# Eight of twelve modulation blocks of a hybrid SSD and gated-MLP layer: from TensorE products to VectorE multiplies with a running sum

## The chip, the cores and the metric

The kernel runs on one core of one Trainium2 chip. The metric is the device time of one execution in microseconds (us), and of several executions the median. The engines are TensorE (PE in the profile; its weight loads are shown apart, as PEld), VectorE (DVE), ScalarE (ACT), GpSimd (POOL), and SyncE (SP), which here only issues DMAs.

## What is computed

One layer of a flow-matching backbone on 1024 latent tokens and 128 context tokens with 1024 channels: a Mamba-2 scan, a spatial gating branch, their merge, and a convolutional FFN. The change concerns the modulation: a condition vector for each of the two kinds of token goes through SiLU and one matrix of 1024 x 6144. The result is cut into six rows of 1024.

```python
mod_ctx = jax.nn.silu(c_ctx)[None, :] @ w_mod[i] + b_mod[i]
mod_lat = jax.nn.silu(c) @ w_mod[i] + b_mod[i]
...
shift1, scale1, gate1, shift2, scale2, gate2 = jnp.split(mod[:, None, :], 6, axis=-1)
h = _rmsnorm(x, lp["norm_mix_pre"]) * (1 + scale1) + shift1
mix, hf, hb = _token_mixer(h, h0_f, h0_b, lp)
x = x + gate1 * _rmsnorm(mix, lp["norm_mix_post"])
h = _rmsnorm(x, lp["norm_ffn_pre"]) * (1 + scale2) + shift2
x = x + gate2 * _rmsnorm(_conv_ffn(h, on_grid, lp), lp["norm_ffn_post"])
```

## The kernel before

All products of large matrices run on TensorE as three products of fp32r parts (high x high, high x low, low x high). Weights come in halves of 128x512 (`wr`, three buffers), each of which ACT casts to its high part (`wh`, L83) and DVE subtracts to its low part (`wl`, L84). A class `Weights` loads and splits them ahead of their use, in the order of one list.

The program has four parts in time: the input projection and the scan, the spatial gating branch, the branch projections with the merge and the output projection, and the FFN. The modulation is cut into twelve blocks of 512 columns. Blocks 0 to 3 (shift1, scale1) are computed at the very start; the change leaves them alone. Blocks 4 to 11 (gate1, shift2, scale2, gate2) are computed in the spatial gating branch, in `mod_step` (L903). It goes as follows, for a block b:

- four DMAs of 512 KB bring its weights (`wmod`, L207) into buffers of the tag `xm`, of which there are four;
- 16 products (L224) with the condition as the stationary operand (`cs`, 32 columns, two of them used) leave partial sums in four groups of rows of a PSUM bank, and ACT copies them out (`modrow`, L228);
- for shift2 and scale2 (`mod_cols`) four transposes (L235) bring the columns onto the partitions, and small DVE operations add the groups up and apply bias and norm weight;
- for the gates (`mod_gate`) two products with a selecting matrix (L253) add the groups up into a row for each kind of token, DVE applies bias and norm weight on one partition (L254, L255), and DMAs write the row to a scratch tensor, `gate_scr`.

Around it, for each half h of the channels of v: one gate unit (72 products into `gps`, three token blocks), then nine token tiles by `v_tile` (L853), each of 24 products into one of the three banks of the pool `pg`, an ACT copy out (L862) and a DVE statistic (L863). The eight halves of the weights of v stay in place for all nine tiles (six of them in `vwh` and `vwl`). Behind every third tile of the second half, `layernorm` normalises three tiles of v (L875). Then come eight u units (`u_unit`, L877), each of three token blocks: 24 products into `gps`, six into `psg` (L881), two DVE operations (L884, L887). L842 is a short product for the branch's bias, early in the stage.

The program is recorded in the order of the code, and a list scheduler then places the instructions of each engine by its own estimates of their durations. So the order in which an engine executes differs from the code's. An engine executes its instructions strictly in the order placed, and an instruction that waits holds up all behind it. SP issues all DMAs, in one such order.

## Time and profile before

| what | value |
|---|---|
| median of 3 runs | 2494.64 us (2494.25 to 2495.19) |
| span of the profiled execution | 2495.0 us |
| mean granted TensorE clock | 0.994 |
| moved by DMA | 322.36 MB, 129 GB/s |

The profiled execution is described by its span alone; it lies 0.4 us above the median. The page gives the busy time of each engine, the chain of work that ended last, and groups of instructions by source line; other views of the trace are the timeline of an engine, tables of windows, and the chain within a window. All times of instructions are in us from the start of the span. A group's row ends with its count, its busy time in us, the mean of one in ns, and the idle time ahead of it with what ended that.

### The profile page before, as it was taken

Reading aid. Unit: us, or ns where it says so; the run is one execution under the profiler, and the core shown is the slowest. Engines: PE = TensorE matmul, PEld = TensorE weight load, DVE = VectorE, ACT = ScalarE, POOL = GpSimd, SP = SyncE. Lnnn points to the kernel's source line nnn. Section 1 sums busy time; section 2 is a strip of 40 time slices with the busy share of each in tenths; the row PEclk is TensorE's granted clock in tenths of the full one; section 3 lists DMA queues with packets and bytes.
Section 4 is the critical chain, followed back from the end, with each engine's and each line's share of the span. In section 5 each row is a group of like instructions: output and inputs, shape, how many; then the busy total and the mean of one; then the engine's idle time right before and its main releaser. Section 6 shows DMA issues by size and latency. Waiting matters only on the chain.

```text
span 2495.0 us, 37933 instructions
## 1 busy us (share of the span) xinstructions
PE 2456.4 (98%) x14237; PEld 2281.7 (91%) x14237; DVE 1795.4 (72%) x3042; ACT 1113.4 (45%) x2124; POOL 26.1 (1%) x82
## 2 busy tenths in 40 slices
PE   7989999999999999999999999999999999999998
PEld 4989999999999997789999998999999999998877
DVE  4768988878868883243455747558999989998554
ACT  4545655655544552211344536444333333334443
POOL 0000000000000000000000000000000000000000
PEclk8999999999999999999999999999999999999999
DMA  6134334434433434531445747542222121214673
GB/s 255 34 99 147 121 125 142 130 95 127 144 94 112 146 118 169 199 105 63 137 153 169 241 155 242 165 147 76 70 72 70 64 72 56 70 62 132 215 246 130
DMA packets 204168, 322.36 MB, mean 129 GB/s; under 512 B 19320, under 2 KB 113400, under 8 KB 203984
## 3 DMA queue, kind: packets, MB, share of 16 engines
q1 hardware_dynamic: 203984, 319.93, 39.2%
q8 instruction: 112, 1.84, 0.3%
q14 instruction: 72, 0.59, 0.1%
HBM read 277.33 MB, written 42.52 MB: 128 GB/s over the span
## 4 chain that ended last, share of the span: by engine, by line
PE 94%; DMA 3%; DVE 1%; ACT 1%; issue 0%; SPq 0%; POOL 0%; DVEq 0%; POOLq 0%; ACTq 0%
PE gps L294 11%; PE gps L296 11%; PE gps L295 11%; PE pup L294 7%; PE pup L295 7%; PE pup L296 7%; PE fo L1132 3%; PE fo L1133 3%; PE fo L1134 3%; PE yo L733 2%; PE pbs L294 2%; PE pbs L295 2%; PE pbs L296 2%; PE yd L737 2%; PE pv L860 1%; PE pv L858 1%
## 5 line engine op out<-in xcount | busy, mean ns | idle before, releaser
L84 DVE TENSOR_TENSOR wl<-wr,wh 128x512 fp32r<-128x512 f32 x544 | 372.2, 689 | 269.4 <-ACT wh L83 256.9
L83 ACT CAST wh<-wr 128x512 fp32r<-128x512 f32 x544 | 333.9, 619 | 492.7 <-PE pup L295 121.6
L294 PE MATMUL gps<-hh,wh 128*128 128x384 f32 x1512 | 518.3, 343 | 0.2 <-ACT pad L349 0.2
L296 PE MATMUL gps<-hh,wl 128*128 128x384 f32 x1512 | 514.2, 340 | 0.0
L295 PE MATMUL gps<-hl,wh 128*128 128x384 f32 x1512 | 513.4, 340 | 0.0
L1120 DVE SCALAR_TENSOR_TENSOR acc<-U,fpar,acc 128x960 f32<-128x960 f32 (+1 forms) x352 | 444.1, 1266 | 16.0 <-ACT acc L1113 8.2
L295 PE MATMUL pup<-h2l,wh 128*128 128x384 f32 x1056 | 353.1, 334 | 0.0
L294 PE MATMUL pup<-h2h,wh 128*128 128x384 f32 x1056 | 352.9, 334 | 0.0
L296 PE MATMUL pup<-h2h,wl 128*128 128x384 f32 x1056 | 352.4, 334 | 0.0
L294 PEld LDWEIGHTS gps<-hh,wh 128*128 128x128 f32 x1512 | 284.7, 188 | 6.7 <-issue 5.9
L296 PEld LDWEIGHTS gps<-hh,wl 128*128 128x128 f32 x1512 | 284.5, 188 | 4.8 <-issue 4.8
L295 PEld LDWEIGHTS gps<-hl,wh 128*128 128x128 f32 x1512 | 284.7, 188 | 4.2 <-issue 4.2
L294 PEld LDWEIGHTS pup<-h2h,wh 128*128 128x128 f32 x1056 | 198.2, 188 | 1.3
L295 PEld LDWEIGHTS pup<-h2l,wh 128*128 128x128 f32 x1056 | 198.2, 188 | 1.3
L296 PEld LDWEIGHTS pup<-h2h,wl 128*128 128x128 f32 x1056 | 198.2, 188 | 0.0
L1102 ACT COPY U<-pup 128x384 f32<-128x384 f32 (+1 forms) x132 | 58.4, 442 | 225.2 <-PE pup L296 225.2
L665 ACT ACTIVATE R<-R,nb 128x128 f32<-128x128 f32 x288 | 93.2, 391 | 130.4 <-DMA R<-acs_scr 120.9
L1132 PE MATMUL fo<-wh,gh 128*128 128x512 f32 x384 | 148.0, 396 | 0.9 <-ACT wh L83 0.9
L1133 PE MATMUL fo<-wh,gl 128*128 128x512 f32 x384 | 148.3, 396 | 0.0
L1134 PE MATMUL fo<-wl,gh 128*128 128x512 f32 x384 | 139.9, 396 | 0.0
L294 PE MATMUL pbs<-ysh,wh 128*128 128x384 f32 x384 | 129.7, 338 | 3.7 <-ACT wh L83 2.2
L296 PE MATMUL pbs<-ysh,wl 128*128 128x384 f32 x384 | 129.5, 337 | 0.1
(302 smaller groups left out, 3939.8 us busy)
## 6 DMA issues: line engine op xcount, KB each, us to landing
wr<-in_w_dn SPq DMA_DIRECT2D x132, 256.0 KB
wr<-in_w_in SPq DMA_DIRECT2D x130, 256.0 KB
R<-acs_scr SPq DMA_DIRECT2D x64, 512.0 KB
wmod<-in_w_mod SPq DMA_DIRECT2D x48, 512.0 KB
wr<-in_w_bs SPq DMA_DIRECT2D x96, 256.0 KB
wr<-in_w_up SPq DMA_DIRECT2D x90, 256.0 KB
EP<-acs_scr SPq DMA_DIRECT2D x128, 128.0 KB
wr<-in_w_bu SPq DMA_DIRECT2D x48, 256.0 KB
```

The lines of the kernel that those rows point to most:

```text
L83: self.nc.scalar.copy(hi, w)
L84: self.nc.vector.tensor_tensor(lo, w, hi.bitcast(F32), op=ALU.subtract)
L294: PE.matmul(ps, lhsT=wh, rhs=xh, start=first and k == 0, stop=False)
L295: PE.matmul(ps, lhsT=wh, rhs=xl, start=False, stop=False)
L296: PE.matmul(ps, lhsT=wl, rhs=xh, start=False, stop=last and k == n - 1)
L665: S.activation(r, r, AF.Identity, bias=nb[:, c, col:col + 1])
L733: PE.matmul(yo[:, d, i, :], lhsT=H[:, k, d, :], rhs=CT[:, 128 * c:128 * c + 128], start=True, stop=True)
L1102: S.copy(u[:, a // 64:b // 64, 1:65], src.rearrange("p (r c) -> p r c", c=64))
L1120: tap = V.scalar_tensor_tensor(av[:, r0:r1], u[:, r0 + dy - 1:r1 + dy - 1, dx:dx + 64], w[i], av[:, r0:r1], op0=ALU.mult, op1=ALU.add)
L1132: PE.matmul(outs[c][h], lhsT=mh[:, cs_], rhs=wh, start=k == 0, stop=False)
L1133: PE.matmul(outs[c][h], lhsT=ml[:, cs_], rhs=wh, start=False, stop=False)
L1134: PE.matmul(outs[c][h], lhsT=mh[:, cs_], rhs=wl, start=False, stop=k == NFF - 1)
```

## The change

The weights of blocks 4 to 11 are given to the kernel transposed: 32 tiles of 128 output channels (on the partitions) by 1024 inputs (`w_modt`), 512 KB each. The two conditions are brought onto all 128 partitions by one broadcast DMA of 1 MB into `cc` and go through SiLU there, on ACT. Each of 64 dot products per partition group is then one DVE instruction: weight tile times condition, with a running sum over the 1024 inputs into one column of `modc` (L247 of the new program). A step (`mod_step`) does one tile, that is two such multiplies, and issues the load of the tile four steps on. One step stands behind every v tile (18 steps) and one behind every token block of the u units, until 32 are done. After each eight, `mod_finish` applies bias and norm weight to eight columns at once; for the two gates, `mod_rows` transposes 16 columns by one product (L259) and writes them to `gate_scr`.

```diff
-    def mod_gate(tile_, ps, pt, b, hs, sel):
...
+    def mod_dot(wt, junk, cc, m):
+        for s in range(2):
+            V.scalar_tensor_tensor(junk if s == 0 else wt, wt, 1.0, cc[:, s, :], op0=ALU.mult, op1=ALU.mult,
+                                   accum_out=modc[:, m, s:s + 1])
+
+    def mod_finish(c0, w=None, one=0.0):
+        m = modc[:, c0:c0 + 8, :]
+        V.tensor_tensor(m, m, par[:, P_BM + c0:P_BM + c0 + 8].unsqueeze(2).to_broadcast([128, 8, 2]), op=ALU.add)
+        if w is not None:
+            V.scalar_tensor_tensor(m, m, one, par[:, w:w + 8].unsqueeze(2).to_broadcast([128, 8, 2]), op0=ALU.add, op1=ALU.mult)
+
+    def mod_rows(ps, room, gi, c0):
+        PE.transpose(ps[:16, :128], modc[:, c0:c0 + 8, :].rearrange("p k s -> p (k s)"), ident)
+        row = room[:16, :128]
+        S.copy(row, ps[:16, :128])
+        for s in range(2):
+            SP.dma_start(gate_scr[2 * gi + s:2 * gi + s + 1, :].rearrange("o (k m) -> (o k) m", m=128), row[s:16:2, :])
...
-    cond_cols(up)
-    sel = up.tile([128, 2, 128], F32, name="sel")
-    SP.dma_start(sel, A["sel"])
+    cc = up.tile([128, 2, 1024], F32, name="cc")
+    SP.dma_start(cc.rearrange("p s k -> p (s k)"), A["cond"].to_broadcast([128, 2048]))
+    S.activation(cc, cc, AF.Silu)
+    junk = rp.tile([128, 1024], F32, tag="gate", name="mjunk")
     mods = []
+    def mod_load1():
+        m = len(mods)
+        if m < 32:
+            wt = xm(f"wmt{m}")
+            SP.dma_start(wt, A["w_modt"][m])
+            mods.append(wt)
...
+            mod_dot(mods[m], junk, cc, 16 + m)
+            mod_load1()
...
         for c in range(NC):
-            if c % 2 and nm < 8 or h == 0 and c == 0:
-                mod_step()
-                mods.append((4 + nm, mod_load(xm, 4 + nm)))
-                nm += 1
             v_tile(h, c, parts)
+            mod_step()
...
-    nc = _bacc.Bacc("TRN2", target_bir_lowering=False, num_devices=1)
+    nc = _bacc.Bacc("TRN2", target_bir_lowering=False, num_devices=1, dynamic_dma_scratch_size=1024)
```

The last pair of lines makes room in on-chip memory for `cc`. The packed parameters grow by 16 columns, and comments are gone from the new text, so line numbers differ by 7 from L84 of the new program on and by more further down.

The order of the instructions is the same in both programs up to the start of the spatial gating branch. From there on it differs, at these places.

**The start of the branch, on DVE and ACT.** These are the rows of DVE from the end of the scan on, before (`vwl` and `wl` are low parts of the weights of v, k tile by k tile; `sb` is the branch's bias):

```order
L592 TENSOR_TENSOR ssq<-ssq,z_9473 128x1152
L215 MEMSET cs 128x256
L84 TENSOR_TENSOR vwl<-wr_9432,vwh 128x512
L84 TENSOR_TENSOR vwl<-wr_9529,vwh 128x512
L84 TENSOR_TENSOR vwl<-wr_9561,vwh 128x512
L844 SCALAR_TENSOR_TENSOR sb<-prs_9593,par,sb 128x128 x4
L84 TENSOR_TENSOR vwl<-wr_9669,vwh 128x512
L844 SCALAR_TENSOR_TENSOR sb<-prs_9599,par,sb 128x128 x4
L84 TENSOR_TENSOR vwl<-wr_9701,vwh 128x512
```

And the rows of DVE at the same place in the changed program:

```order
L85 TENSOR_TENSOR vwl<-wr_9561,vwh 128x512
L851 SCALAR_TENSOR_TENSOR sb<-prs_9593,par,sb 128x128 x4
L851 SCALAR_TENSOR_TENSOR sb<-prs_9599,par,sb 128x128 x4
L247 SCALAR_TENSOR_TENSOR mjunk,modc<-wmt_9613,cc 128x1024
L85 TENSOR_TENSOR vwl<-wr_9676,vwh 128x512
L85 TENSOR_TENSOR vwl<-wr_9708,vwh 128x512
L247 SCALAR_TENSOR_TENSOR wmt_9613,modc<-wmt_9613,cc 128x1024
L247 SCALAR_TENSOR_TENSOR mjunk,modc<-wmt_9615,cc 128x1024
L85 TENSOR_TENSOR vwl<-wr_9715,vwh 128x512
L85 TENSOR_TENSOR wl_9730<-wr_9719,wh_9729 128x512
```

The split of the fourth k tile, and every split behind it, now has multiplies ahead of it. On ACT the changed program has these rows there:

```order
L84 CAST vwh<-wr_9561 128x512
L908 ACT_TABLE_LOAD
L908 ACTIVATE cc<-cc 128x2048
L84 CAST vwh<-wr_9676 128x512
L84 CAST vwh<-wr_9708 128x512
```

The SiLU of `cc`, which needs the broadcast, stands ahead of the cast of the fourth k tile; before, a SiLU of 16 columns of `par` stood there, whose input had been there since the start of the program.

**The same place on SP.** The DMAs issued before, from the first modulation weights on (`gb_scr` takes gate rows out, `wsT`, `sb` and `sel` are small operands, `wr` the weights of v):

```order
L207 DMA wmod_9734<-in_w_mod 128x1024
L604 DMA gb_scr<-gt 128x384 x2
L207 DMA wmod_9736<-in_w_mod 128x1024
L207 DMA wmod_9738<-in_w_mod 128x1024
L836 DMA wsT<-in_sgu_w 128x1024
L838 DMA sb<-in_sgu_b 128x1024
L900 DMA sel<-in_sel 128x256
L71 DMA wr_9669<-in_w_v 128x512
```

And those of the changed program:

```order
L916 DMA wmt_9613<-in_w_modt 128x1024
L916 DMA wmt_9615<-in_w_modt 128x1024
L916 DMA wmt_9617<-in_w_modt 128x1024
L916 DMA wmt_9619<-in_w_modt 128x1024
L611 DMA gb_scr<-gt 128x384
L843 DMA wsT<-in_sgu_w 128x1024
L845 DMA sb<-in_sgu_b 128x1024
L907 DMA cc<-in_cond 128x2048
L72 DMA wr_9676<-in_w_v 128x512
```

One more load of modulation weights and the broadcast of `cc` now stand ahead of the load of the fourth k tile.

**The second half of v, on DVE.** The splits of its weights stood before behind statistics and single rows of the gates; this is the changed program from the first of these splits on:

```order
L85 TENSOR_TENSOR vwl<-wr_10038,vwh 128x512
L247 SCALAR_TENSOR_TENSOR wmt_10220,modc<-wmt_10220,cc 128x1024
L247 SCALAR_TENSOR_TENSOR mjunk,modc<-wmt_10251,cc 128x1024
L870 BN_STATS stat<-vtok 128x6
L85 TENSOR_TENSOR vwl<-wr_10095,vwh 128x512
L85 TENSOR_TENSOR vwl<-wr_10127,vwh 128x512
L247 SCALAR_TENSOR_TENSOR wmt_10251,modc<-wmt_10251,cc 128x1024
L247 SCALAR_TENSOR_TENSOR mjunk,modc<-wmt_10291,cc 128x1024
L85 TENSOR_TENSOR vwl<-wr_10134,vwh 128x512
L253 TENSOR_TENSOR modc<-modc,par 128x16
L85 TENSOR_TENSOR wl_10149<-wr_10138,wh_10148 128x512
```

Multiplies now stand between the splits as well as ahead of them. The scheduler has moved the multiplies forward against the code: all 64 stand ahead of the last `layernorm`, so none is left among the u units.

## The prediction

> **What bounds the kernel now.** I read the page first: busy time by engine, then the chain that ended last.

> ```profile
> span 2495.0 us, 37933 instructions
> ...
> PE 2456.4 (98%) x14237; PEld 2281.7 (91%) x14237; DVE 1795.4 (72%) x3042; ACT 1113.4 (45%) x2124; POOL 26.1 (1%) x82
> ...
> PE 94%; DMA 3%; DVE 1%; ACT 1%; issue 0%; SPq 0%; POOL 0%; DVEq 0%; POOLq 0%; ACTq 0%
> ```

> TensorE carries 94% of the chain, so a microsecond taken off TensorE counts unless a wait takes its place. The profiled execution spans 2495.0 us and the median of the runs is 2494.64 us: nothing but 0.4 us separates them, and I subtract from the median. The share of busy time is an average, so the next view is the table of windows over the stage that is edited: from the first product of v (956.65) to the end of the first spatial product (1103.76), and the eight u units behind it.

> ```profile
> 956.65:1103.76 147.11, 147.11 (x828) 109.30 (x828) 48.15 (x95) 30.41 (x52) 2.55 (x3) 1.00 0.51 176
> 1103.76:1218.00 114.24, 114.24 (x706) 114.24 (x705) 44.46 (x76) 16.43 (x30) 0.00 (x0) 1.00 0.22 73
> ```

> Columns: length, then busy time of PE, weight load, DVE, ACT, POOL, granted clock, DMA share, GB/s. TensorE is never idle in either stretch. DVE works 48 of 147 us. That is the room into which the change moves the modulation.

> **What is removed.** Eight blocks of modulation leave TensorE. The chain inside the window 955 to 1110 (155 us) gives their shares, and three pieces of it show what one block does to its neighbours.

> ```profile
> by line: PE pv L860 22.1%; PE pv L858 21.9%; PE pv L859 21.6%; PE pm L224 10.9%; PE gps L295 5.4%; PE gps L294 5.3%; PE gps L296 5.3%; PE pmt L253 2.2%; PE pm L253 2.2%; PE prs L842 1.2%; PE pmt L235 1.1%; PE psg L881 0.9%
> ...
> 1042.63 1.86 PE pm L224 x32
> 1044.49 0.43 PE pv L858
> 1044.92 0.24 PE pv L859
> ```

> L224, L253 (twice) and L235 are 10.9 + 2.2 + 2.2 + 1.1 = 16.4% of 155 us, **25.4 us**. Each run of L224 also delays the product behind it, 0.43 us in place of 0.23: 19 such places, **3.8 us**. Removed: **29.2 us**. The two products that are added (the 16-row transposes of L259) have the nearest row in L235: 1.1% of 155 us over 16 records is 0.11 us each, with 0.2 us behind them at most; I take **0.3 us** for both, between 0.2 and 0.6.

> **The cover that goes at the start.** The first part of the stage was short of weights, and modulation filled the hole. Timelines of DVE, ACT, PE and SP:

> ```profile
> 957.88 0.69 DVE L84 TENSOR_TENSOR vwl<-wr,vwh 128x512 fp32r<-128x512 f32 x1 [2.02 <-ACT vwh L83]
> ...
> 967.63 0.68 DVE L84 TENSOR_TENSOR vwl<-wr,vwh 128x512 fp32r<-128x512 f32 x1
> ...
> 966.31 0.62 ACT L83 CAST vwh<-wr 128x512 fp32r<-128x512 f32 x1 [6.93 <-DMA wr<-in_w_v]
> ...
> 956.30 0.33 PE L295 MATMUL gps<-hl,wh 128*128 128x384 f32 x1
> 956.47 0.33 PE L296 MATMUL gps<-hh,wl 128*128 128x384 f32 x1
> ...
> 960.77 0.39 PE L858 MATMUL pv<-vwh,hh 128*128 128x512 f32 x1
> 961.00 0.39 PE L859 MATMUL pv<-vwh,hl 128*128 128x512 f32 x1
> ...
> 964.42 1.07 PE L224 MATMUL pm<-wmod,cs 128*32 128x256 f32 x16
> 965.42 1.98 PE L842 MATMUL prs<-wsT,cst 128*128 128x512 f32 x4
> ```

> The third k tile was split at 958.6, the fourth only at 967.6, because its load landed at about 966.2. A product of v starts 0.23 us behind the one before it (960.77, 961.00; 0.2275 over many), one of a projection unit 0.17 (956.30, 956.47; 0.1735). With three v tiles open TensorE has 27 products of 0.2275 us (956.65 to 962.8) and L842 (1.9 us): dry at **964.7** once L224 is gone.

> The fourth k tile also comes later. ACT's cast of it now stands behind the SiLU of cc, which waits for cc's transfer. KB ahead of the point that matters, by the issues of 950 to 980:

> ```profile
> wmod<-in_w_mod SPq DMA_DIRECT2D x5, 512.0 KB
> wr<-in_w_v SPq DMA_DIRECT2D x8, 256.0 KB
> yssd_scr<-X SPq DMA_DIRECT2D x1, 576.5 KB
> gb_scr<-gt SPq DMA_DIRECT2D x3, 192.0 KB
> wsT<-in_sgu_w SPq DMA_DIRECT2D x1, 512.0 KB
> sb<-in_sgu_b SPq DMA_DIRECT2D x1, 512.0 KB
> sel<-in_sel SPq DMA_DIRECT2D x1, 128.0 KB
> ...
> 954.00:966.30 12.30, 12.30 (x70) 8.64 (x69) 1.99 (x3) 3.55 (x7) 0.00 (x0) 1.00 1.01 355
> ```

> Before, through the fourth k tile: 576.5 + 3 x 512 + 2 x 192 + 512 + 512 + 128 + 256 = 3904 KB, at full DMA share. After, through cc (1024 KB): 576.5 + 4 x 512 + 192 + 512 + 512 + 1024 = 4864 KB. The 960 KB more, 983,000 bytes, take 2.8 us at 355 GB/s: cc lands at about 969.0. A SiLU of 2048 columns is 1.97 us, extrapolated from these two:

> ```profile
> L591 ACT ACTIVATE z<-X 128x1024 f32<-128x1024 f32 x16 | 16.9, 1058 | 9.7 <-DVE X L590 9.7
> ...
> L520 ACT ACTIVATE pad<-z 128x1152 f32<-128x1152 f32 x16 | 18.7, 1172 | 1.3
> ```

> Then the cast, 0.62 us. TensorE resumes at 971.7: a stall of **7.0 us**. Its bounds are 4 us (cc as early as the old load) and 10 us (a broadcast of 1 MB at half the rate). Afterwards TensorE needs 5 x 9 x 0.2275 = 10.2 us for the five remaining k tiles; DVE's splits, with multiplies between them, reach the last at about 981, in step with it. One more cover is lost behind the three tiles, where L253 ran while ACT emptied the first bank: **0.4 us**, most of a 0.59 us copy.

> A long pause also costs clock, as the start of this kernel shows:

> ```profile
> 18.00:20.00 2.00, 0.36 (x2) 0.30 (x2) 0.79 (x3) 2.00 (x5) 0.00 (x0) 0.99 1.02 416
> 20.00:22.00 2.00, 2.00 (x8) 1.77 (x6) 1.14 (x4) 1.83 (x4) 0.00 (x0) 0.50 1.04 416
> 22.00:24.00 2.00, 1.76 (x7) 1.42 (x7) 1.03 (x3) 0.00 (x0) 0.86 (x1) 0.66 1.03 410
> ```

> After a stretch with TensorE 0.36 of 2 us busy, the granted clock was 0.50 for 2 us and 0.66 for the next 2. Lost are 0.50 x 2 + 0.34 x 2 = **1.7 us**; bounds 0 and twice that.

> **What is added on DVE.** 64 multiplies with a running sum, 128x1024. No row has the sum. The nearest:

> ```profile
> L590 DVE TENSOR_TENSOR X<-X,z 128x1024 f32<-128x1024 f32 x16 | 19.5, 1218 | 0.1
> ...
> L521 DVE SCALAR_TENSOR_TENSOR z<-pad,z 128x1152 f32<-128x1152 f32 x16 | 21.6, 1352 | 1.2 <-ACT pad L520 1.2
> ...
> 969.26 1.28 DVE L84 TENSOR_TENSOR vwl<-wr,vwh 128x512 fp32r<-128x512 f32 x2
> ...
> 20.60 0.19 ACT L337 ACTIVATION_READ_ACCUMULATOR xj<-x 128x1 f32 x1
> 20.69 1.05 ACT L337 ACTIVATE xj<-x 128x1024 f32<-128x1024 f32 x1
> ```

> L521 is the same operation without a sum, 1.17 ns a column, like the plain product of L590: **1.22 us** for 1024. Two in a row overlap by 0.09 us (1.28 for two of 0.69). On ACT a sum adds a read that moves the next start by 0.09 us (20.60 to 20.69). I take 1.22 + 0.09 = **1.31 us**; lower bound 1.13 (overlapped, sum free), upper 1.50 (1.22, plus the whole 0.19 us read, plus 0.09 for the wait between the two of a pair). 64 x 1.31 = 84 us into 99 us of idle DVE: it fits, but only just, because the stage gets shorter.

> So DVE's row order is added up from 971.0, with 0.69 us a split or statistic:

> ```profile
> L863 DVE BATCH_NORM_STATS2 stat<-vtok 128x6 f32<-128x512 f32 x18 | 12.4, 692 | 46.2 <-ACT vtok L862 46.2
> ...
> L875 DVE TENSOR_SCALAR vtok<-vtok,mv,rv 128x1024 f32<-128x1024 f32 x9 | 6.8, 808 | 3.0 <-POOL rv L265 3.0
> ```

> Two points decide. The eighth k tile of v's second half stands behind 35 multiplies, 15 splits and 9 statistics: 45.9 + 16.6 + 0.5 = 63 us, at 1034. TensorE wants it at 981.9 + 0.4 + 1.7 + six v tiles of 5.46 (24 products) + 0.2 + a gate unit of 12.5 (72 products) + 4.8 (seven k tiles) = 1034. No loss. The last normalised tile of vtok stands behind all 64, 19 splits, 18 statistics, 9 times 0.81, 4 us of small ones and a wait of about 1 us for POOL, 1092 to 1093; TensorE wants it for the third block of the first u unit at 1092.4. I take **0.5 us**. Behind that DVE is half idle again (44 of 114 us). The 32 loads of weights are 512 KB each as before, and every wait on the SP queue is for a DVE row already passed. The room for DMA descriptors that the program gives up belongs to no queue that the page lists; I price it at nothing from either side.

> **The sum.** 29.2 - 7.0 - 1.7 - 0.4 - 0.3 - 0.5 = **19.3 us** saved; 2494.64 - 19.3 = **2475 us**.

> **The rivals.**

> *DVE becomes the bound* (slower). Above 1.31 us, each 0.01 us of a multiply adds 0.64 us at the last vtok tile, on which TensorE waits. At 1.31 + 19.3/64 = 1.61 us the gain is gone; beyond it the kernel is slower than before. If the second fp32 source costs a second pass of 1.07 us (1024 columns at 1.04), a multiply is 2.38 us, 68 us more: 2543 us. Against it: L521 and L590 have two fp32 sources at full rate, and L863, a reduction, takes for 512 columns what a split of 512 takes (0.69 us). Only the sum is unseen. Chance 0.10. [...]

> *The stall at the start is longer*: cc's transfer, a broadcast, or loads queued behind it take another 5 to 8 us. For it: the DMA share is 1.01 there. Against: sb is a broadcast too, and the rate held. 2480 to 2485 us, chance 0.15.

> *The stall hardly appears*, because cc lands with the first weights: 29.2 - 4 - 0.7 = 24.5 us, 2470 us. Chance 0.08.

> *The gain is given back* at later transfers, or TensorE did not lose what the chain says:

> ```profile
> 1361.07 4.22 DMA yrs<-yssd_scr
> ...
> 1366.82 6.08 DMA wr<-in_w_bs
> ```

> These waits of the whole chain end on loads released by buffers that come free in program order, so they should move up with the rest. About 2494 us, chance 0.05.

> **How the numbers follow.** Forecast 0.62, with 2471 to 2480 as its own range. The range of 2468 to 2489 takes in the longer stall and a multiply of up to 1.5 us (12 us later, 2487). A difference of 0.2%, 5 us, is about what a measurement of this kernel can tell from none: faster 0.85 (0.62 + 0.15 + 0.08), same 0.05, slower 0.10.

> **What would show it.** The multiply's mean in the group of L247, with its read of the sum (1.2 to 1.4). TensorE idle ahead of the fourth k tile, 6 to 8 us, released by ACT, and a granted clock of 0.5 behind it. TensorE not waiting for DVE at L259 or at the first u unit; a wait there in tens of microseconds would mean the first rival. u units at the old 14.6 us each and later stages earlier by one constant. It would be wrong if TensorE idled in the v tiles at large.

## The result, and the profile after

| | before | after |
|---|---|---|
| time, median of 4 runs each, us | 2494.91 (2494.25 to 2499.63) | 2475.29 (2471.90 to 2481.27) |
| ratio, 95% interval | | 0.9921 (0.9905 to 0.9937) |
| the edited stage in the profiled run, us | 258.90 | 239.56 |

The kernel is 19.6 us faster, by 0.8%. The forecast of 2475 us held. The profiled execution of the changed kernel is its slowest (2481.27 us, span 2479.3). Its page has the same shape as before; DVE now works 75% of the span:

```profile
span 2479.3 us, 37397 instructions
...
PE 2428.8 (98%) x13951; PEld 2271.1 (92%) x13951; DVE 1854.7 (75%) x3150; ACT 1110.4 (45%) x2118; POOL 27.0 (1%) x82
...
PE 89%; DMA 5%; DVE 3%; ACT 1%; issue 1%; SPq 1%; POOL 0%; DVEq 0%; POOLq 0%; ACTq 0%
```

Spans are a poor measure of this edit: the profiled executions of the kernels shown here reach the first product of v anywhere between 954.5 and 963.2 us, for work ahead of it that is the same or nearly so. I therefore measure the edited **stage**, from the first product of v to the end of the last spatial product. First the table of windows over the stage, before and after. Columns: length, busy time of PE, weight load, DVE, ACT and POOL, granted clock, DMA share, GB/s.

```profile
956.65:1215.55 258.90, 258.90 (x1518) 221.09 (x1518) 90.19 (x166) 44.41 (x76) 2.55 (x3) 1.00 0.38 131
```

```profile
960.82:1200.38 239.56, 232.64 (x1232) 212.77 (x1232) 150.27 (x275) 41.69 (x70) 3.48 (x3) 0.99 0.44 145
```

The stage lost 258.90 - 239.56 = **19.3 us**, and DVE gained 60 us of work (90.2 to 150.3, after losing its own part of the old modulation). Two things in the second row are new: TensorE idles 239.56 - 232.64 = **6.9 us**, and the clock is not 1.00. The spans differ by 15.7 us only, since the profiled execution of the changed kernel enters the stage 4.2 us later (960.82, not 956.65) and needs 0.6 us less behind it.

Where TensorE idles is told by its own timeline in the changed kernel, by the chain of waits from 955 to 985 us (start, duration, what) and by the timelines of DVE and of ACT there:

```profile
969.20 1.98 PE L849 MATMUL prs<-wsT,cst 128*128 128x512 f32 x4 [2.05 <-DMA wsT<-in_sgu_w]
975.77 0.79 PE L865 MATMUL pv<-vwh,hh 128*128 128x512 f32 x1 [4.59 <-ACT vwh L84]
```

```profile
962.14 11.14 DMA cc<-in_cond
973.30 1.91 ACT cc L908
975.21 0.52 ACT vwh L84
```

```profile
970.51 2.16 DVE L851 SCALAR_TENSOR_TENSOR sb<-prs,par,sb 128x128 f32<-128x128 f32 x8 [7.77 <-DMA sb<-in_sgu_b]
975.24 1.23 DVE L247 SCALAR_TENSOR_TENSOR mjunk<-wmt,cc 128x1024 f32<-128x1024 f32 x1 [2.57 <-ACT cc L908]
```

```profile
973.30 1.91 ACT L908 ACTIVATE cc<-cc 128x2048 f32<-128x2048 f32 x1 [9.98 <-DMA cc<-in_cond]
975.12 1.70 ACT L84 CAST vwh<-wr 128x512 fp32r<-128x512 f32 x3
```

The cast of the fourth weight tile (L84, which is L83 of the kernel before) starts when the SiLU of cc ends, and the SiLU when cc has landed. TensorE takes up the fourth tile 14.95 us after the first product of v; 27 products of 0.2275 us and the 1.9 us of prs fill 8.05 of these. The stall is **6.9 us** (forecast 7.0). As idle time it shows in two pieces: 2.05 us ahead of prs, where TensorE waits for wsT, and 4.59 us for the cast; 0.28 us more, a wait for a bank, stand 28 us into the stage. During the second piece, at about 974.2, the granted clock is halved:

```profile
973.00:975.00 2.00, 0.00 (x0) 0.00 (x0) 0.00 (x0) 1.70 (x1) 0.00 (x0) 0.81 1.02 387
975.00:977.00 2.00, 1.23 (x3) 1.04 (x4) 1.76 (x4) 1.82 (x4) 0.00 (x0) 0.50 0.07 25
977.00:979.00 2.00, 2.00 (x6) 1.51 (x6) 2.00 (x5) 0.00 (x0) 0.00 (x0) 0.50 0.46 98
979.00:981.00 2.00, 2.00 (x6) 1.57 (x5) 2.00 (x4) 0.62 (x1) 0.00 (x0) 0.50 0.82 238
981.00:983.00 2.00, 2.00 (x10) 1.60 (x9) 2.00 (x4) 0.62 (x1) 0.00 (x0) 0.99 0.75 277
```

Six products in 2 us at half clock, ten at full clock. From 975.77, where TensorE resumes, to 981.05 twelve products start, most of them 0.427 us apart; at 0.2275 us they would fill 2.73 of these 5.28 us. The half clock costs 2.55 us, or **2.6 us** in round numbers. Last, the multiply, in the groups of DVE between 960 and 1095 us (busy, mean ns, idle before and what ended it), and two rows of DVE's timeline:

```profile
L247 DVE SCALAR_TENSOR_TENSOR mjunk<-wmt,cc 128x1024 f32<-128x1024 f32 x32 | 39.0, 1220 | 2.6 <-ACT cc L908 2.6
L247 DVE SCALAR_TENSOR_TENSOR wmt<-wmt,cc 128x1024 f32<-128x1024 f32 x32 | 38.9, 1215 | 0.2
...
L247 DVE DVE_READ_ACCUMULATOR wmt<-wmt,cc 128x1 f32 x32 | 2.6, 82 | 0.0
```

```profile
978.75 1.22 DVE L247 SCALAR_TENSOR_TENSOR mjunk<-wmt,cc 128x1024 f32<-128x1024 f32 x1
979.89 0.08 DVE L247 DVE_READ_ACCUMULATOR mjunk<-wmt,cc 128x1 f32 x1
```

A multiply lasts 1.22 us and the next instruction starts 1.14 us behind its start (978.75 to 979.89). The read of the sum, 0.08 us, stands at that same moment and delays nothing.

### The profile page after: what moved, and what is told of

Its sections match the earlier page's. It is cut to its first block, busy times and chain, and to the rows that moved or that the text cites. A ratio compares the mean times of both kernels' runs of the same rounds, so it can differ in the third digit from the quotient of the medians.

```text
span 2479.3 us, 37397 instructions
## 1 busy us (share of the span) xinstructions
PE 2428.8 (98%) x13951; PEld 2271.1 (92%) x13951; DVE 1854.7 (75%) x3150; ACT 1110.4 (45%) x2118; POOL 27.0 (1%) x82
## 4 chain that ended last, share of the span: by engine, by line
PE 89%; DMA 5%; DVE 3%; ACT 1%; issue 1%; SPq 1%; POOL 0%; DVEq 0%; POOLq 0%; ACTq 0%
PE gps L301 10%; PE gps L302 10%; PE gps L303 10%; PE pup L302 7%; PE pup L301 7%; PE pup L303 7%; PE fo L1152 4%; PE fo L1154 4%; PE fo L1153 4%; PE pbs L301 2%; PE pbs L303 2%; PE pbs L302 2%; PE yo L740 2%; PE yd L744 2%; DMA R<-acs_scr 2%; PE pv L865 1%
## 5 line engine op out<-in xcount | busy, mean ns | idle before, releaser
L84 ACT CAST wh<-wr 128x512 fp32r<-128x512 f32 x544 | 333.8, 619 | 473.8 <-PE pup L302 121.6
## 6 DMA issues: line engine op xcount, KB each, us to landing
wr<-in_w_dn SPq DMA_DIRECT2D x132, 256.0 KB, 2.8
wr<-in_w_in SPq DMA_DIRECT2D x130, 256.0 KB, 2.8
R<-acs_scr SPq DMA_DIRECT2D x64, 512.0 KB, 4.4
wr<-in_w_bs SPq DMA_DIRECT2D x96, 256.0 KB, 3.5
wr<-in_w_up SPq DMA_DIRECT2D x90, 256.0 KB, 2.6
EP<-acs_scr SPq DMA_DIRECT2D x128, 128.0 KB, 3.2
wmt<-in_w_modt SPq DMA_DIRECT2D x32, 512.0 KB, 3.8
wr<-in_w_bu SPq DMA_DIRECT2D x48, 256.0 KB, 3.0
```

Of the source, the lines that this page charges most:

```text
L84: self.nc.scalar.copy(hi, w)
```

## The experiments

Two theories were open. **One**: what the change gains less than the 29 us of modulation is all lost at the start of the stage, through the order of the loads, and DVE costs nothing. **Rivals**: TensorE had less to lose than the chain said; the transfers would hold TensorE in any order; DVE is as near to its bound as the forecast had it. The table has the stage, the start of the fourth tile's products behind the first product of v, the stretches of half clock in the first 30 us by the trace's record of the granted clock, and the time (one run, except where a range or an interval is given in the text). The kernel before was timed again beside them: 2494.9 and 2495.5 us as medians, and 2500.2 us in the one run beside "multiplies twice".

| kernel | stage us | fourth tile | half clock | time us |
|---|---|---|---|---|
| before | 258.9 | 10.3 | none | 2494.9 |
| after | 239.6 | 15.0 | 6.8 | 2475.3 |
| cc early | 236.1 | 12.2 | 3.4 | 2477.7 |
| late loads | 234.0 | 9.7 | none | 2468.7 |
| cc early, late loads | 235.2 | 7.9 | 3.4 | 2474.2 |
| cc early, loads behind all | **229.3** | 7.9 | none | **2466.2** |
| filler in the pause | 237.3 | 14.4 | none | 2475.1 |
| no modulation | 231.2 | 8.6 | none | 2464.7 |
| no sum | 237.4 | 14.0 | 3.4 | 2476.2 |
| multiplies twice, free order | 237.8 | 15.0 | 3.4 | 2481.4 |
| half of them twice, order forced | 261.4 | 14.8 | 3.4 + 3.4 | 2501.9 |

**No modulation.** What is there to gain?

```diff
-    cc = up.tile([128, 2, 1024], F32, name="cc")
-    SP.dma_start(cc.rearrange("p s k -> p (s k)"), A["cond"].to_broadcast([128, 2048]))
-    S.activation(cc, cc, AF.Silu)
+    V.memset(modc[:, 16:48, :], 0.5)
...
-            mod_dot(mods[m], junk, cc, 16 + m)
-            mod_load1()
...
-    for _ in range(NXM):
-        mod_load1()
```

> Leaves out the eight modulation blocks: no loads of their weights, no cc, no multiplies; their results are 0.5 throughout. Theory A (29.2 us of TensorE's stage were modulation and 0.3 us come back as two small products; what the changed kernel gains less goes to the start): stage 258.9 - 28.9 = 230 us, 229 to 232, no wait of TensorE at the start. Rival B (TensorE did not lose what the chain says, and the stall is elsewhere): stage 236 to 240 us, as in the changed kernel.

```profile
954.54:1185.76 231.22, 230.15 (x1232) 210.95 (x1231) 78.33 (x140) 38.31 (x68) 2.55 (x3) 1.00 0.22 72
```

231.2 us, with 1.1 us of TensorE idle in it: 27.7 us less than before, 28.7 without the idle time. Theory A. TensorE did lose what the chain said, within 0.5 us, and 8.3 us of it are missing in the changed kernel.

**cc early.** The tile of cc moves to a pool that lasts, and its load and SiLU are tied behind steps 13 and 15 of the scan. `queue_behind` orders issues on one engine, without a wait; `marks` holds the instructions to stand behind, of the scan and, for the first multiply, the last one of the branch's bias (`sb`).

```diff
-    SP.dma_start(cc.rearrange("p s k -> p (s k)"), A["cond"].to_broadcast([128, 2048]))
-    S.activation(cc, cc, AF.Silu)
+    cload = SP.dma_start(cc.rearrange("p s k -> p (s k)"), A["cond"].to_broadcast([128, 2048]))
+    queue_behind(cload, marks[13, "SP"])
+    silu = S.activation(cc, cc, AF.Silu)
+    queue_behind(silu, marks[15, "ACT"])
...
+            if m == 16 and s == 0:
+                queue_behind(dot, marks["sb"])
```

> cc is loaded and put through SiLU during the scan, behind step 13's loads; everything else stays where it is in the changed kernel, the four first loads of modulation weights too. Stage = first product of v to last product of the spatial gating (239.6 us in the changed kernel, 258.9 before). Theory A (the fourth weight tile of v is late because ACT's cast of it stands behind cc's transfer and its SiLU): without them 1024 KB less are ahead, 2.9 us at 355 GB/s, and no SiLU of 1.9 us stands before the cast, so the product of the fourth tile starts about 4 us sooner, 11 us behind the first product of v in place of 15.0, and the pause is too short for the half clock (2.6 us): stage 232 to 236 us. Rival B (the transfers share one rate, so something else that is loaded there holds TensorE as long): the fourth tile starts 14 to 15 us behind the first product and the stage stays at 239 to 240 us.

The timeline of TensorE in this kernel:

```profile
969.11 3.68 PE L853 MATMUL prs<-wsT,cst 128*128 128x512 f32 x4 [2.36 <-DMA wsT<-in_sgu_w]
972.59 0.52 PE L869 MATMUL pv<-vwh,hh 128*128 128x512 f32 x1
...
975.75 0.50 PE L871 MATMUL pv<-vwl,hh 128*128 128x512 f32 x1 [1.48 <-DVE vwl L85]
```

The stage is 236.1 us, just outside what theory A gave (232 to 236), and far from rival B's 239. The fourth tile starts 2.8 us sooner, not 4. What I had left out: the first 2.4 us of the pause are a wait for wsT, behind the same four loads of modulation weights. That wait was enough for 3.4 us of half clock, and prs took 3.68 us in place of 1.98. A little later TensorE waits 1.48 us for the low part of the fourth tile: DVE's split of it stands behind the first multiply (1.14 us). So DVE is not quite free there once cc is out of the way.

**Late loads.** cc stays; the four first loads of modulation weights (2048 KB) go behind the fourth tile of v.

```diff
-    for _ in range(NXM):
-        mod_load1()
...
+        if h == 0:
+            for _ in range(NXM):
+                queue_behind(mod_load1(), W.issued[v_at[0] + 3])
```

> Only the four first loads of modulation weights are moved, behind the fourth weight tile of v; cc stays where it is in the changed kernel. 2048 KB less are ahead of cc, 5.9 us at 355 GB/s. Theory A (the data ahead on the queue sets the stall): the product of the fourth tile starts 9 to 10 us behind the first product of v in place of 15.0, the half clock is gone, stage 231 to 234 us. But the multiplies then start no sooner than in the changed kernel while TensorE is 8 us ahead: if DVE's margin is only the 7 us that its waits for TensorE showed, TensorE waits up to 2 us for DVE at the first u unit. Rival B (the SiLU and its table load alone hold the cast, whatever is loaded): fourth tile at 13 to 15 us, stage 238 to 240 us.

TensorE's waits in the first 30 us of the stage:

```profile
966.42 0.50 PE L865 MATMUL pv<-vwh,hh 128*128 128x512 f32 x1 [1.69 <-ACT vwh L84]
...
974.16 0.50 PE L865 MATMUL pv<-wh,hh 128*128 128x512 f32 x1 [1.31 <-ACT wh L84]
...
979.28 0.50 PE L865 MATMUL pv<-vwh,hh 128*128 128x512 f32 x1 [0.43 <-ACT vtok L869]
```

Theory A: the fourth tile 9.7 us behind the first product, no half clock, 234.0 us. So the bytes ahead of the load on the queue set this stall, whether they are cc (15.0 to 12.2 us without its 1024 KB and its SiLU) or weights (15.0 to 9.7 us without their 2048 KB). No wait for DVE appeared. What is left (3.4 us of idle) are 1.7 us for the fourth tile itself, whose cast still stands behind cc and its SiLU, 1.3 for a later tile and 0.4 for a bank.

**cc early, late loads.** Both, the four loads behind the sixth tile of v.

```diff
+                queue_behind(mod_load1(), W.issued[v_at[0] + 5])
```

> As the run with cc early, and the first four loads of modulation weights (2048 KB) stand behind the sixth weight tile of v on the queue of SP. Theory A: no stall of TensorE for the fourth tile, no half clock; the stage loses the 7.5 us of the stall and 2.6 us of half clock of the changed kernel: 229 to 231 us, TIME about 2465 us, ratio to the kernel before 0.988. DVE starts its multiplies 2 to 5 us sooner, so the margin at the last normalised tile stays. Rival B (DVE becomes late because the weights come late, or the stall comes back elsewhere in the first v tiles): stage 235 to 240 us, 2470 to 2475 us.

Ratio to the kernel before 0.9912 (0.9898 to 0.9925): not separable from the change itself. The stall for the fourth tile is gone (7.9 us), yet the stage is 235.2 us: rival B, and ACT's timeline names the place.

```profile
977.61 1.96 ACT L84 CAST wh<-wr 128x512 fp32r<-128x512 f32 x3 [6.47 <-DMA wr<-in_w_v]
984.36 0.62 ACT L84 CAST wh<-wr 128x512 fp32r<-128x512 f32 x1 [4.80 <-DMA wr<-in_w_in]
984.88 1.55 ACT L873 COPY vtok<-pv 128x512 f32<-128x512 f32 x3
```

The 2 MB now stand ahead of the seventh tile, so its cast waits 6.5 us. Then a cast for the next gate unit waits 4.8 us on ACT with the copies of finished v tiles queued behind it, and TensorE for their banks.

**cc early, loads behind all.** As the last, with the four loads behind all eight tiles of v's first half and the two of the next gate unit.

```diff
+                queue_behind(mod_load1(), W.issued[v_at[0] + 9])
```

> As the run with cc early and late loads, but the first four loads of modulation weights stand behind all eight weight tiles of v's first half and the two of the next gate unit, not behind the sixth. In that run the 7th tile's cast waited 6.5 us for its transfer behind 2048 KB of modulation weights, and a copy of a v tile 4.8 us behind a cast for the gate unit. Theory A (the queue's order alone made those waits): no wait of TensorE for weights in the first half of v; stage 228 to 231 us, TIME 2466 to 2469 us. Theory B (DVE's margin is only 7 us, and the multiplies start as late as in the changed kernel, 14 us behind the first product, while TensorE is 10 us ahead): a wait of TensorE for DVE of 2 to 4 us in the second half of v or at the first u unit; stage 231 to 234 us. Rival C (the rate of the transfers keeps TensorE short whatever the order): 235 us and more.

```profile
960.96:1190.28 229.32, 229.32 (x1232) 211.25 (x1232) 149.46 (x275) 38.61 (x68) 2.55 (x3) 1.00 0.45 146
```

TensorE is busy for the whole stage at a clock of 1.00, with DVE's 149 us of work beside it. 2466.16 us, ratio 0.9877 (0.9860 to 0.9893): below the interval of the change, so this version beats both kernels. Theory B, a wait for DVE, did not come. The stage is 10.2 us shorter than the change's, which is the cost of the start: 6.9 us of idle TensorE and 3.3 us more of busy time, 2.6 of them at half clock.

**Filler in the pause.** Is the half clock made by the pause? Four products more, of the same result, keep TensorE at work there.

```diff
+        for _ in range(3):
-        PE.matmul(ps, lhsT=ones, rhs=wsT[:, 4 * hb:4 * hb + 4, :], start=True, stop=True)
+            PE.matmul(ps, lhsT=ones, rhs=wsT[:, 4 * hb:4 * hb + 4, :], start=True, stop=True)
```

> The product of the row sums of the spatial weights is made three times in each half, four products of about 1 us more, with the same result; they stand where TensorE waits for the fourth weight tile. Theory A (the half clock behind the pause comes from the pause itself): TensorE resumes at the same time as in the changed kernel, 15.0 us behind the first product of v, at full clock, and the stage is 2.6 us shorter, 237 us. Rival B (the half clock comes from something else there, such as the transfers): the granted clock is 0.5 for 7 us all the same, stage 239 to 240 us. Rival C (the filler is too long and delays the fourth tile): stage above 240 us.

First two rows of TensorE's timeline, then the windows from 970 to 976 us:

```profile
966.30 5.42 PE L850 MATMUL prs<-wsT,cst 128*128 128x512 f32 x12 [1.87 <-DMA wsT<-in_sgu_w]
972.52 0.50 PE L866 MATMUL pv<-vwh,hh 128*128 128x512 f32 x1 [0.80 <-ACT vwh L84]
```

```profile
970.00:972.00 2.00, 1.71 (x4) 0.41 (x3) 0.55 (x3) 1.96 (x2) 0.00 (x0) 1.00 1.03 389
972.00:974.00 2.00, 1.48 (x6) 1.05 (x6) 2.00 (x7) 1.58 (x3) 0.00 (x0) 1.00 0.08 29
974.00:976.00 2.00, 1.49 (x7) 1.11 (x7) 2.00 (x5) 0.00 (x0) 0.00 (x0) 1.00 0.25 24
```

Theory A: the clock stays at 1.00, with the transfers at 389 GB/s (387 in the pause of the changed kernel, from 973 to 975), and the stage is 2.2 us shorter, of which the fourth tile explains 0.5 at most (14.4 us, not 15.0). Here the pause makes the half clock: 1.00 with it filled, 0.50 behind it without.

**No sum.** Does the running sum cost anything?

```diff
-            V.scalar_tensor_tensor(junk if s == 0 else wt, wt, 1.0, cc[:, s, :], op0=ALU.mult, op1=ALU.mult,
-                                   accum_out=modc[:, m, s:s + 1])
+            V.scalar_tensor_tensor(junk if s == 0 else wt, wt, 1.0, cc[:, s, :], op0=ALU.mult, op1=ALU.mult)
...
+    V.memset(modc[:, 16:48, :], 0.5)
```

> The 64 multiplies are made without the running sum; the sums are left out and the eight blocks' values are 0.5 before bias and norm weight. Theory A (the sum costs only a read that starts behind its own multiply and lies beside the next one's start): without it the starts of two multiplies in a row are 1.12 to 1.15 us apart, as with it (1.145). Rival B (the read delays the next start by its 0.08 us): 1.06 to 1.08 us. Rival C (the sum slows the pass itself): a multiply below 1.15 us in place of 1.22. In all three the stage stays at 239 to 240 us, since DVE isn't late.

```profile
992.31 1.23 DVE L247 SCALAR_TENSOR_TENSOR wmt<-wmt,cc 128x1024 f32<-128x1024 f32 x1
993.45 1.22 DVE L247 SCALAR_TENSOR_TENSOR mjunk<-wmt,cc 128x1024 f32<-128x1024 f32 x1
```

Over 37 such pairs the median from start to start is 1.136 us; with the sum it is 1.144 (36 pairs). The duration is the same, 1.22 us. Theory A: the sum costs 0.01 us. The stage, 237.4 us, fell outside the 239 to 240 that I had written: its stall was 1 us shorter and its half clock 3.4 us in place of 6.8, and neither concerns the sum.

**DVE, twice.** First a forced order: the first condition's multiply is made twice, and the last block's first normalised tile stands behind all 96 multiplies.

```diff
-            V.scalar_tensor_tensor(junk if s == 0 else wt, wt, 1.0, cc[:, s, :], op0=ALU.mult, op1=ALU.mult,
-                                   accum_out=modc[:, m, s:s + 1])
+            for _ in range(2 - s):
+                marks["dot"] = V.scalar_tensor_tensor(junk if s == 0 else wt, wt, 1.0, cc[:, s, :], op0=ALU.mult, op1=ALU.mult,
+                                                      accum_out=modc[:, m, s:s + 1])
...
+            if c == 6:
+                queue_behind(norm, marks["dot"])
...
+            if h and c == 8:
+                while mod_step.n < 32:
+                    mod_step()
```

> The multiply of the first condition is made twice (32 more multiplies, 36.6 us of DVE at 1.145 us), and the last block's first normalised tile of vtok stands behind all of them on DVE. Theory A (DVE is the next bound behind a margin of some 7 us: 3.6 and 0.3 us of waits for TensorE and 3.2 us from the last normalisation to its use): TensorE waits for DVE about 29 us at the third block of the first u unit; stage 269 us, slower than the kernel before (258.9 us). That is the first rival of the prediction with its point of decision: 29.8 us more DVE work was to undo the gain. Rival B (DVE's work hides wherever it stands, since DVE is half idle in the u units): stage 240 to 243 us.

The timelines of TensorE and DVE at the third block of the first u unit:

```profile
1127.28 2.05 PE L892 MATMUL psg<-wsT,vtok 128*128 128x128 f32 x8 [21.21 <-DVE modc L255]
```

```profile
1125.17 1.22 DVE L249 SCALAR_TENSOR_TENSOR wmt<-wmt,cc 128x1024 f32<-128x1024 f32 x1
...
1126.32 0.81 DVE L884 TENSOR_SCALAR vtok<-vtok,mv,rv 128x1024 f32<-128x1024 f32 x1
```

The product waits 21.2 us and starts when the tile is normalised (1127.13; the profile names a small DVE operation of that moment as the releaser), and the kernel is slower than before: stage 261.4 us, 2501.9 us. The size that I gave, 29 us, was too large. The last of the three tiles that the product needs came 36.0 us later than in the changed kernel (164.5 behind the first product of v, not 128.5). There TensorE wants it only at 136.6, a room of 8.1 us, and here TensorE had other products until 143.4. In the wait the clock was halved too (0.95 on average over the stage, 0.99 in the changed kernel's); it came back 4.35 us behind the end of the wait, a stretch that the table's first 30 us leave out.

Then all multiplies twice, 73 us more on DVE, and no order forced:

```diff
+            if s == 1:
+                for d in range(2):
+                    V.scalar_tensor_tensor(junk, wt, 1.0, cc[:, d, :], op0=ALU.mult, op1=ALU.mult, accum_out=modc[:, m, d:d + 1])
```

> Both multiplies of every step are made twice (64 more, 73 us of DVE), with no order forced: 71 of the 128 stand ahead of the last normalised tile of vtok, 57 lie between the u units' own operations. Theory A (where DVE's work stands decides, not how much it is): 7 multiplies more ahead of the last normalisation are 8 us, of which 3.6 us fill a wait for TensorE and 8 us is the room up to the product that wants it, so nothing is late there; in a u unit 7 multiplies of 1.145 us and 5.7 us of its own are 13.9 of 14.1 us. Stage 239 to 242 us. Rival B (DVE too full in the u units: each spatial block's result waits behind a multiply and TensorE for its bank): the u units grow by 1 to 3 us each, stage 248 to 263 us. Rival C (73 us of work without room): stage above 290 us.

```profile
960.17:1197.92 237.75, 231.09 (x1231) 212.01 (x1231) 217.28 (x399) 41.27 (x69) 2.55 (x3) 0.99 0.44 142
```

DVE is busy 217 of 238 us and the stage is no longer than the change's. Theory A, a little below its range, mostly because the half clock was 3.4 us. The time of that one run, 2481.4 us, is high, and so is the 2500.2 us of the kernel before beside it. Behind the stage it has 1281.7 us, 2.8 more than the changed kernel; 1.65 of them are a wait of TensorE for a split on DVE, 39 us behind the stage. Whether the added multiplies, the last of which ends 2.3 us behind the stage, cause it was not tried. So 37 us of DVE work ahead of one tile cost the stage 22, and 73 us that lie mostly between the u units cost it nothing.

## Why the prediction was right

| term | forecast us | measured us |
|---|---|---|
| modulation removed, less the two products added | 28.9 | 29.6 (258.90 - 229.32) |
| stall at the start | 7.0 | 6.9 |
| half clock and lost bank cover | 2.1 | 3.3 (the rest of 10.2) |
| DVE late | 0.5 | 0 |
| net | 19.3 | 19.3 |

- **Removed work.** The forecast, read from the chain's shares and the delays behind each run of L224, was 0.7 us short by the stage with no wait left in it, and 0.2 us over by the kernel without modulation (28.7). The u units did not change: from the first to the last spatial product 112.6 us before and 112.7 after.
- **The stall** was right in size and mechanism: cc's transfer, SiLU, cast, in that order. cc landed at 973.3; the forecast of 969.0, moved by the 4.2 us that this execution entered the stage later, is 973.2. The wait for wsT was not in the working: prs was to fill TensorE until it ran dry, and instead TensorE waited 2.05 us ahead of it, so only 4.59 us of the stall were released by ACT, not 6 to 8. This made no difference to the end of the stall, and cost time only once cc was out of the way.
- **Half clock.** Right in kind, too small by the stretch: 1.7 us was taken from a place with 2 us of half clock and 2 of 0.66, which is one stretch of 3.4 us; here it lasted 6.8 us, 5.2 of them under work, and cost 2.6, inside the bounds of 0 to 3.4. In other runs of the same stall it lasted 3.4. Which of the two came went with where the pause lay (last section): 6.8 us behind 4.59 us for the cast, 3.4 us behind 4.5 and 4.2 us, so the pause's length alone leaves two values. The wait for a bank, the other part of this term, is there (0.28 us of idle; forecast 0.4); the 0.7 us of longer busy time that the half clock leaves over were not taken apart.
- **The multiply** was the term most off: 1.31 us taken, 1.14 measured, the lower bound of 1.13. I carried ACT's read of a sum over to DVE, where it costs 0.01 us. The 64 x 0.17 = 11 us were not gained, because DVE was already within its cover. They turned "fits, but only just" into a room of 8.1 us at the last normalised tile.
- **DVE as the bound.** In the forced order TensorE did wait for DVE, 21.2 us, at the place named; the multiply just wasn't dear enough. The second pass of 1.07 us in the first rival was a supposition of mine, and no run shows it: with its running sum the multiply takes 1.22 us for 1024 columns, not 2.38, beside 1218 ns of the plain product of L590. The point of decision of 1.61 us was about right: the room of 8.1 us and the gain of 19.3, over 64 multiplies, are 0.43 us each above 1.14, or 1.57 us, as an estimate for the changed kernel's own order; with the forced order's other products, until 143.4, it would be 1.67. The waits of 1.48 us (cc early) and 0.51 us (filler) for a split show a second place where DVE can be late, the first tiles of v, which the working had as "in step".
- **Nothing was given back.** Behind the stage 1279.5 us were left before and 1278.9 after.

The misses, 0.7 us of removed work and 0.5 of DVE on one side, 1.2 of clock and bank on the other, cancelled. That the sum agrees to the tenth is luck, all the more as the runs of one kernel scatter by several microseconds; the forecast is right by its large terms, the 29 us and the 7 us.

## What to carry to other kernels

Work that is taken off an engine may have been covering something: here a late load. The wait for it, with the half clock that followed, then took 10 of 29 us, and it came back through the order of one DMA queue. So add up the bytes ahead of each load that someone waits for, and put the new loads behind all of those, not behind the first one that hurts. On the engine that takes the work over, ask which of its results another engine waits for and what stands ahead of that one; its busy share said little here (217 of 238 us busy cost the stage nothing, 37 us ahead of one tile cost it 22).

## What the runs showed of the hardware that was not expected

- In the traces of the kernel before and of the changed one every record of the granted clock but the last, which the end of the program cuts off, lasts a multiple of one step of 3.413 us: a stretch of half clock lasts 3.41 or 6.83 us before, and 3.41, 6.83 or 10.24 us in the changed kernel. The stretches in the table are of one step or two. What came ahead of each of these in the first 30 us of the stage is one step in which TensorE had little work. These are steps of the changed kernel (the first four), of cc early and of cc early with late loads, with the columns of the windows above:

```profile
967.39:970.81 3.42, 1.61 (x4) 0.68 (x4) 0.30 (x2) 0.00 (x0) 0.00 (x0) 1.00 1.05 408
970.81:974.22 3.41, 0.37 (x1) 0.00 (x0) 1.86 (x8) 0.92 (x1) 0.00 (x0) 1.00 1.00 366
974.22:977.63 3.41, 1.86 (x4) 1.49 (x5) 2.39 (x5) 2.60 (x4) 0.00 (x0) 0.50 0.26 97
977.63:981.05 3.42, 3.42 (x9) 2.63 (x8) 3.42 (x7) 0.62 (x1) 0.00 (x0) 0.50 0.77 204
...
965.84:969.25 3.41, 1.05 (x6) 0.55 (x5) 0.00 (x0) 0.00 (x0) 0.00 (x0) 1.00 1.03 379
...
982.55:985.96 3.41, 1.50 (x7) 0.96 (x6) 2.43 (x6) 1.60 (x4) 0.00 (x0) 1.00 0.90 310
```

- The running sum on DVE shows as a separate read of 0.08 us that overlaps the end of its multiply (978.75 + 1.22 = 979.97, the read from 979.89), and costs 0.01 us: 1.144 us from start to start with it, 1.136 without.
- The load of cc and its SiLU inside the scan may cost the scan something: the kernel with cc early and late loads gained 4.4 us in the stage and 1.1 in time. The last kernel, with the same early cc, gained 10.2 in the stage and 9.1 in time, so a cost of microseconds is unlikely; it was not tried apart.
